# A decoder layer on one core: the MLP's norm transposes by two row tiles with pairs of column blocks, and six shared load places

## The chip, the cores and the metric

One core of a Trainium2 chip runs the whole kernel. The metric is device time in microseconds (us) of one execution, the median of several runs. TensorE (PE) multiplies and transposes, VectorE (DVE), ScalarE (ACT) and GpSimd (POOL) do elementwise work, and SyncE (SP) only issues transfers; POOL and ACT issue some too. Each engine and each queue works through its own instructions in order.

## The reference, cut to what matters

One decoder layer for 2048 tokens of width 1024, all in float32. Four token mixers (a gated MLP, a state-space layer, a gated recurrence and an attention with forget gates) come first and take about the first 1000 us; the change doesn't touch them. What follows them is

```python
x = x + group_rms_norm(y, mix_norm_g) @ w_out
h = rms_norm(x, norm2_g)
x = x + square(relu(h @ w_mlp_in)) @ w_mlp_out     # 1024 -> 4096 -> 1024
return rms_norm(x, final_g)
```

where rms_norm(x, g) is x / sqrt(mean(x^2) + 1e-6) * g by rows.

## The kernel before

A tile framework gives the instructions their order on each engine, from the program's order and from which tile buffers are free, and it adds the waits. In the stages ahead of the MLP, TensorE keeps the program's order; in the MLP (class MLP) all engines take the framework's.

**Precision.** Every matmul operand is split into a high and a low part (split, L54 on ACT and L58 on DVE): the high part is a cast, the low part the difference. A product is three matmuls: high x high, high x low, low x high (L1556 to L1558 and L1581 to L1583).

**Products by blocks.** Both MLP products use a seven-product scheme on 2 x 2 blocks (tables FIRST and SECOND): the operands of each of the seven are single blocks or sums and differences of two blocks. Where two are needed, both are loaded into one tile of [128, 2, 512] and POOL adds or subtracts them in place (united, L1484). For the first product five of the seven weights (all but numbers 4 and 3) and most of the token operands are such pairs. For the second product the sums of weights are written to memory beforehand (weight_sums), all but one, number 1.

**Steps.** The tokens are done in two halves of 1024 rows, the later rows first ("first half" below means the one done first). In each half there are two column parts (c) of the hidden width; in each part an IN block, seven products of 8 steps (order 1, 4, 5, 7, 3, 2, 6), and an OUT block, seven of 8 (order 3, 5, 6, 1, 2, 4, 7). So a half has 4 x 56 = 224 steps, each of 12 matmuls of 128x128 by 128x512. A step's weights are asked for two steps ahead (make(n + AHEAD)); in steps 1 to 5 of an IN product the token operands of the next product are loaded and split (tokens_side, four tiles).

**prep.** The MLP's first product wants the normalised tokens transposed. prep does this for one half: it loads x1 tiles of 128 rows x 1024 (L1462), ACT sums the squares (L1464), a chain of 12 small DVE operations gives the reciprocal root (rsqrt_, L28 to L36), DVE scales the rows in place (L1469), TensorE transposes blocks of 128x128 (L50), ACT moves four of them (a piece) at once out of PSUM and multiplies with the norm's weight (L1477) into one of two ht buffers, and SP stores that as hT (L1478). It does four row tiles at a time and one block of 128 columns (k) per transposed piece. It is a generator: every yield hands back to the caller. For the first half it runs beside the output projection (wout_jobs), one call per turn of it from the fifth on; the rest follows when those turns are used up. For the second half it runs inside the first half's steps: from step 11 on, one call in every second step (`if n % 2 and n > 10: next(more, None)`). Four tiles take 14 calls: one for the loads, six more until the first transposes, then one per k.

**Places.** Loads that need a pair, the token operands and the x1 tiles of prep all take their SBUF tile from one pool, m_raw, of 4 KB per partition and five places:

```python
self.raw = P("m_raw", 5)
xt = self.raw.tile([128, D], F32, tag="raw", name="h")           # prep
raw = self.raw.tile([128, 2, 512], F32, tag="raw", name="raw")   # load
```

Single weights have a pool of their own (m_rw, five places of 2 KB). A pair's place comes free when its high and low parts have been made (L54, L58); an x1 tile's place when its last block has been transposed.

**The end of a half.** finish (L1592) multiplies the rows of a finished row tile with the reciprocal root and with gf, the final norm's weight spread over all partitions. gf has a pool of its own and is loaded once, ahead of the MLP.

The functions that the diff touches and what calls them:

Of the kernel before, what the change touches and what calls it, by code (L numbers as in the profile page):

```python
# [1425 lines left out]
class MLP:  # L1426
# [4 lines left out]
    def __init__(self, tc, cst, final_g, x1, hT, w1, w2, S2, out, T=2048):  # L1431
        self.tc, self.nc, self.cst, self.x1, self.hT, self.w1, self.w2, self.out, self.T = tc, tc.nc, cst, x1, hT, w1, w2, out, T
        self.final_g, self.S2 = final_g, S2
        self.D, self.FF = w1.shape
        self.KD = self.D // 128
        self.HT = 1024
        self.NC = 2
        self.NP = self.FF // 128 // self.NC // 2
        self.es = ExitStack()
        self.P = lambda n, b, **k: self.es.enter_context(tc.tile_pool(name=n, bufs=b, reuse_waits="tile", **k))  # L1440
        P = self.P
        self.bp = P("m_b", 2)
        self.raw = P("m_raw", 5)
        self.rw = P("m_rw", 5)
        self.wp = P("m_w", 4)
        self.htp = P("m_ht", 2)
        self.sm = P("m_sm", 2)
        self.jkp = P("m_jk", 1)
        self.ps_i = P("m_psi", 3, space=PSUM)
        self.halves = list(reversed(range(T // self.HT)))  # L1450

    def prep(self, half):

        nc, D = self.nc, self.D
        for q in range(self.HT // 512):
            ss = self.sm.tile([128, 4], F32, tag="ss", name="ss")
            rs = self.sm.tile([128, 4], F32, tag="rs", name="rs")
            xs = []
            for j in range(4):
                r0 = half * self.HT + q * 512 + j * 128  # L1460
                xt = self.raw.tile([128, D], F32, tag="raw", name="h")
                nc.sync.dma_start(out=xt, in_=self.x1[r0 // 128])  # L1462
                jk = self.jkp.tile([128, D], BF16, tag="jk", name="jk")
                nc.scalar.activation(out=jk, in_=xt, func=AF.Square, accum_out=ss[:, j:j + 1])  # L1464
                xs.append(xt)
            yield
            rsqrt_(nc, self.sm, rs, ss, 1.0 / D, "n2")
            for j in range(4):
                nc.vector.tensor_scalar(out=xs[j], in0=xs[j], scalar1=rs[:, j:j + 1], scalar2=None, op0=MUL)  # L1469
            for _ in range(5):  # L1470
                yield
            for k in range(self.KD):
                pt = self.ps_i.tile([128, 512], F32, tag="pi", name="tp")
                for j, h in enumerate(xs):
                    transpose(nc, out=pt[:, j * 128:(j + 1) * 128], in_=h[:, k * 128:(k + 1) * 128], ident=self.cst["ident"])
                ht = self.htp.tile([128, 512], F32, tag="ht", name="ht")
                nc.scalar.activation(out=ht, in_=pt, func=AF.Copy, scale=self.cst["g2"][:, k:k + 1])  # L1477
                nc.sync.dma_start(out=self.hT[k][half * 2 + q], in_=ht)  # L1478
                yield

    def united(self, raw, sign):
# [12 lines left out]
    def tokens_side(self, half, i):  # L1494

        a, b, sign = FIRST[i][1]
        bh = self.bp.tile([128, 4, 512], F32R, tag="bh", name="bh")
        bl = self.bp.tile([128, 4, 512], F32R, tag="bl", name="bl")
        yield bh, bl
        for k in range(4):  # L1500
            raw = self.load([self.hT[4 * x[0] + k][half * 2 + x[1]] for x in (a, b) if x])
            split(self.nc, bh[:, k], bl[:, k], self.united(raw, sign if b else 0))
            yield

# [91 lines left out]
    def run(self):  # L1596
        nc, P, NP = self.nc, self.P, self.NP

        P("m_pad", 1).tile([128, 32], F32, tag="pad", name="pad")
        self.cp = P("m_c", 1)  # L1600
        self.sp = P("m_s", 3)
        self.shp = P("m_sh", 4)
        accp = P("m_acc", 1)
        gp = P("m_gf", 1)
        ps_o = P("m_pso", 5, space=PSUM)
        self.C, self.acc = {}, {}
        ends = {}
        for order, table, n in ((IN_ORDER, FIRST, 0), (OUT_ORDER, SECOND, 1)):
            seen, last = {}, {}
            for i in order:  # L1610
                for blk, _ in table[i][2]:
                    seen.setdefault(blk, i)
                    last[blk] = i
            ends[n] = {i: [b for b in seen if seen[b] == i] for i in order}, {i: [b for b in last if last[b] == i] for i in order}
        steps = [(half, c, out, i, p) for half in self.halves for c in range(self.NC) for out in range(2)
                 for i in (OUT_ORDER if out else IN_ORDER) for p in range(NP)]
        made, sides = {}, {}
        groups = [s[:4] for s in steps if s[4] == 0 and not s[2]]

        def side(n):  # L1620
            if n < len(groups):
                half, _, _, i = groups[n]
                g = self.tokens_side(half, i)
                sides[groups[n]] = next(g)
                return g
            return iter(())

        def make(n):
            if n >= len(steps):
                return  # L1630
            half, c, out, i, p = steps[n]
            if not out:
                made[n] = (self.first_weight(c, i, p),)
            else:
                made[n] = self.second_weight(c, i, p), self.hidden_side(i, p)

        gf = gp.tile([128, self.D], F32, tag="gf", name="gf")
        nc.sync.dma_start(out=gf, in_=self.final_g.partition_broadcast(128))
        for _ in side(0):
            pass  # L1640
        for n in range(AHEAD):
            make(n)
        nxt, more, part = 1, iter(()), iter(())
        sums = weight_sums(self.tc, self.w2, self.S2, 1, SP, nc.sync)
        for n, (half, c, out, i, p) in enumerate(steps):
            if c == 0 and not out and i == IN_ORDER[0] and p == 0:
                k = self.halves.index(half) + 1
                more = self.prep(self.halves[k]) if k < len(self.halves) else iter(())
            if c == 0 and not out and i == IN_ORDER[3]:
                self.acc[p] = accp.tile([128, self.D], F32, tag=f"acc{p}", name="acc")  # L1650
                with behind(self.tc, SP):
                    nc.sync.dma_start(out=self.acc[p], in_=self.x1[half * self.HT // 128 + p])
            if n % 2 and n > 10:
                next(more, None)
            if n > 7 * NP and n % 3 == 0:
                next(sums, None)
            make(n + AHEAD)
            if not out and p == 1:
                part = side(nxt)
                nxt += 1  # L1660
            if not out and 1 <= p < 6:
                next(part, None)
            got = made.pop(n)
            first, last = (e[i] for e in ends[out])
            if not out:
                self.product_in(i, p, got[0], sides[half, c, out, i], first, last)
                continue
            if p == 0:
                po = [ps_o.tile([128, 512], F32, tag="po", name="po") for _ in range(4)]
            self.product_out(p, *got, po)  # L1670
            if p == NP - 1:
                for t in range(4):
                    for (rt, d), sign in SECOND[i][2]:
                        self.gather(self.acc[4 * rt + t][:, d * 512:(d + 1) * 512], po[t], sign)
                    if c == self.NC - 1:
                        for rt in range(2):

                            if (rt, 0) in last and all((rt, 1) not in e for e in later(ends[1][1], i)) or \
                                    (rt, 1) in last and all((rt, 0) not in e for e in later(ends[1][1], i)):
                                self.finish(half, 4 * rt + t, gf)  # L1680
        self.es.close()
# [17 lines left out]
def hybrid_kernel(tc, A, out, T=2048):  # L1699
    nc = tc.nc  # L1700
    with ExitStack() as top:
# [8 lines left out]
                 zb=dp.tile([T, 256], F32, name="zb"), qk=dp.tile([2, 4, 2, 64, T], F32, name="qk"),  # L1710
                 v=dp.tile([T, 4, 2, 64], F32, name="v"), ys=dp.tile([T, 1024], F32, name="ys"),
                 negc=dp.tile([4, T], F32, name="negc"), x1=[dp.tile([128, 1024], F32, name=f"x1_{t}") for t in range(T // 128)],
                 hT=[[dp.tile([128, 512], F32, name=f"hT_{k}_{q}") for q in range(T // 512)] for k in range(8)])
        S2 = {(i, c): dp.tile([1024, 512], F32, name=f"s2_{i}{c}") for i in OUT_ORDER if SECOND[i][1][1] and i != 1 for c in range(2)}
        D5 = s5_scratch(dp)
        r8 = cp.tile([128, NPR], F32, name="r8")
# [115 lines left out]
```

## Time and profile before

| what | us |
|---|---|
| median of 3 runs | 2665.54 (2664.99 to 2669.57) |
| the profiled execution | 2665.58 |
| its span | 2663.4 |
| MLP: first product_in matmul | at 1127.78 |
| TensorE busy, of the span | 2248.9 |

Times in rows count from the span's start. An instruction's row gives its engine, its line in the kernel, what it writes and reads, and in square brackets how long its engine had stood idle before it and what ended that. PEclk, the granted clock, is the share of TensorE's full 2.4 GHz. The DMA share is the mean busy share of the core's 16 DMA engines.

### The profile page before, as it was taken

To read this page: it belongs to the slowest core of one execution; us is meant where nothing else is said; L and a number is where in the kernel's file an instruction comes from. 1 tells how busy PE (TensorE), PEld (TensorE's weight loads), DVE (VectorE), ACT (ScalarE), POOL (GpSimd) and SP (SyncE) were. 2 spreads that over 40 slices of the span, in tenths; PEclk is the share of its full clock that TensorE was granted. 3 is DMA by queue.
4 is the path that set the end of the run, shared out by engine and by line. 5 is a ranking of instruction groups with operands and counts; after the bars stand their busy time and mean duration, and the time that the engine had idled before them with its cause. 6 is when DMAs were issued, how large, how long until landed. Compare 5 with 4: busy or idle time off the path is not lost.

```text
span 2663.4 us, 32203 instructions
## 1 busy us (share of the span) xinstructions
PE 2248.9 (84%) x10077; PEld 1809.3 (68%) x10077; DVE 1699.7 (64%) x3776; ACT 1171.6 (44%) x2351; POOL 895.8 (34%) x956
## 2 busy tenths in 40 slices
PE   6788986985898978784474598999989999999997
PEld 5666765764776867563353376887877788788885
DVE  6776654753566755451152288687978779768797
ACT  4323443342555643341242243566445663356543
POOL 2133343230000011221111155346643467345561
PEclk9899998997899989896786698999999999999998
DMA  7434566445465546853442398687338963377423
GB/s 174 133 76 111 144 145 175 111 126 169 147 182 185 161 143 212 301 172 95 138 139 80 120 262 209 180 238 227 111 99 248 288 215 120 102 220 230 143 87 107
DMA packets 397147, 434.52 MB, mean 163 GB/s; under 512 B 42864, under 2 KB 277392, under 8 KB 396720
## 3 DMA queue, kind: packets, MB, share of 16 engines
q1 hardware_dynamic: 357840, 352.64, 43.8%
q0 software_dynamic: 30400, 65.15, 9.6%
q10 hardware_dynamic: 8736, 14.68, 1.7%
q8 instruction: 80, 1.31, 0.2%
q14 instruction: 91, 0.75, 0.1%
HBM read 369.30 MB, written 96.57 MB: 175 GB/s over the span
## 4 chain that ended last, share of the span: by engine, by line
PE 44%; DMA 15%; DVE 6%; issue 5%; POOL 5%; ACT 3%; SPq 2%; POOLq 0%; ACTq 0%; DVEq 0%
PE po L1581 6%; PE po L1582 6%; PE po L1583 6%; PE pi L1556 5%; PE pi L1558 5%; PE pi L1557 5%; DMA raw<-in_w_mlp_in_dram 5%; POOL raw L1484 3%; DMA q<-qk 3%; DVE wl L58 2%; DMA raw<-hT 2%; PE s L1087 2%; PE t L50 2%; PE po L1362 1%; PE po L1364 1%
## 5 line engine op out<-in xcount | busy, mean ns | idle before, releaser
L1484 POOL TENSOR_TENSOR raw<-raw 128x512 f32<-128x512 f32 x272 | 388.3, 1434 | 570.5 <-DMA raw<-in_w_mlp_in_dram 364.4
L1556 PE MATMUL pi<-bh,wh 128*128 128x512 f32 x896 | 378.0, 422 | 179.6 <-ACT wh L54 172.2
L58 DVE TENSOR_TENSOR wl<-raw,wh 128x512 fp32r<-128x512 f32 x448 | 403.7, 907 | 169.7 <-ACT wh L54 168.1
L1558 PE MATMUL pi<-bh,wl 128*128 128x512 f32 x896 | 372.9, 416 | 3.9 <-DVE wl L58 3.9
L1581 PE MATMUL po<-wh,sh 128*128 128x512 f32 x896 | 355.0, 396 | 20.0 <-DVE acc L1572 19.8
L1557 PE MATMUL pi<-bl,wh 128*128 128x512 f32 x896 | 370.7, 414 | 0.0
L54 ACT CAST wh<-raw 128x512 fp32r<-128x512 f32 x448 | 275.2, 616 | 211.8 <-POOL raw L1484 139.2
L1582 PE MATMUL po<-wl,sh 128*128 128x512 f32 x896 | 353.3, 394 | 4.5 <-DVE wl L58 4.5
L1583 PE MATMUL po<-wh,sl 128*128 128x512 f32 x896 | 350.1, 394 | 0.1
L1543 POOL TENSOR_TENSOR s<-c 128x512 f32<-128x512 f32 x160 | 254.4, 1604 | 270.6 <-DVE sl L58 243.2
L1556 PEld LDWEIGHTS pi<-bh,wh 128*128 128x128 f32 x896 | 181.8, 203 | 235.4 <-ACT wh L54 187.9
L58 DVE TENSOR_TENSOR sl<-s,sh 128x512 fp32r<-128x512 f32 x160 | 188.8, 1188 | 47.0 <-ACT sh L54 44.0
L1558 PEld LDWEIGHTS pi<-bh,wl 128*128 128x128 f32 x896 | 180.8, 202 | 52.7 <-DVE wl L58 14.7
L1581 PEld LDWEIGHTS po<-wh,sh 128*128 128x128 f32 x896 | 170.8, 191 | 60.4 <-DVE acc L1572 23.1
L54 ACT CAST sh<-s 128x512 fp32r<-128x512 f32 x160 | 99.4, 621 | 251.8 <-PE po L1582 202.7
L1557 PEld LDWEIGHTS pi<-bl,wh 128*128 128x128 f32 x896 | 182.2, 203 | 37.8
L1582 PEld LDWEIGHTS po<-wl,sh 128*128 128x128 f32 x896 | 171.1, 191 | 40.4 <-DVE wl L58 5.4
L1583 PEld LDWEIGHTS po<-wh,sl 128*128 128x128 f32 x896 | 170.8, 191 | 36.7 <-DVE sl L58 0.4
L436 PE MATMUL z<-wh,hl 128*128 128x512 f32 (+1 forms) x384 | 152.3, 397 | 16.7 <-ACT hl L54 8.5
L1572 DVE TENSOR_TENSOR c<-pi,c 128x512 f32<-128x512 f32 x128 | 87.5, 684 | 106.2 <-PE pi L1558 106.2
L58 DVE TENSOR_TENSOR bl<-raw,bh 128x512 fp32r<-128x512 f32 x112 | 101.9, 919 | 68.6 <-ACT bh L54 66.6
L438 PE MATMUL z<-wh,hl 128*128 128x512 f32 (+1 forms) x384 | 143.4, 373 | 1.6 <-DVE hl L58 1.6
(358 smaller groups left out, 4314.4 us busy)
## 6 DMA issues: line engine op xcount, KB each, us to landing
raw<-in_w_mlp_in_dram SPq DMA_DIRECT2D x384, 256.0 KB
raw<-hT SPq DMA_DIRECT2D x192, 256.0 KB
raw<-s SPq DMA_DIRECT2D x128, 256.0 KB
raw<-in_w_mlp_out_dram SPq DMA_DIRECT2D x128, 256.0 KB
x<-in_x_dram SPq DMA_DIRECT2D x32, 512.0 KB
s<-in_w_mlp_out_dram POOLq DMA_DIRECT2D x32, 512.0 KB, 8.1
x<-x POOLq DMA_DIRECT2D x31, 512.0 KB, 5.7
raw<-in_w_in_dram SPq DMA_DIRECT2D x32, 256.0 KB
```

The source lines that it names most:

```text
L54: nc.scalar.copy(out=hi, in_=src)
L58: nc.vector.tensor_tensor(out=lo, in0=src, in1=hi.bitcast(F32), op=SUB)
L436: nc.tensor.matmul(pz, lhsT=hi[:, k, sl], rhs=wh, start=(k == 0), stop=False)
L438: nc.tensor.matmul(pz, lhsT=lo[:, k, sl], rhs=wh, start=False, stop=(k == 7))
L1484: self.nc.gpsimd.tensor_tensor(out=raw[:, 0], in0=raw[:, 0], in1=raw[:, 1], op=ADD if sign > 0 else SUB)
L1543: self.nc.gpsimd.tensor_tensor(out=s, in0=src, in1=self.C[b[1], b[0], p], op=ADD if sign > 0 else SUB)
L1556: nc.tensor.matmul(pt, lhsT=wh[:, sl], rhs=bh[:, k], start=(k == 0), stop=False)
L1557: nc.tensor.matmul(pt, lhsT=wh[:, sl], rhs=bl[:, k], start=False, stop=False)
L1558: nc.tensor.matmul(pt, lhsT=wl[:, sl], rhs=bh[:, k], start=False, stop=(k == 3))
L1581: nc.tensor.matmul(po[t], lhsT=sh[:, ts], rhs=vh, start=(p == 0), stop=False)
L1582: nc.tensor.matmul(po[t], lhsT=sh[:, ts], rhs=vl, start=False, stop=False)
L1583: nc.tensor.matmul(po[t], lhsT=sl[:, ts], rhs=vh, start=False, stop=(p == self.NP - 1))
```

## The change

prep takes two row tiles at a time, and two blocks of columns per transposed piece: a piece is still four transposes and 128x512 elements, and a half still has 16 of them. The piece leaves PSUM through DVE, as a product with the norm's weight spread along the tokens. hT is laid out by 512 tokens and pairs of k, so that a piece is stored with rows of 256 tokens. Two tiles take 8 calls: one for the loads, three more until the first transposes, then one per k pair. The pool m_raw has six places, and gf has no pool any more: in each half it is loaded into a place of m_raw at the first step of the sixth OUT product of the second column part.

```diff
-        self.raw = P("m_raw", 5)
+        self.raw = P("m_raw", 6)
...
     def prep(self, half):
         nc, D = self.nc, self.D
-        for q in range(self.HT // 512):
-            ss = self.sm.tile([128, 4], F32, tag="ss", name="ss")
-            rs = self.sm.tile([128, 4], F32, tag="rs", name="rs")
+        g2 = self.cst["g2"].rearrange("p (k o) -> p k o", o=1)
+        for m in range(self.HT // 256):
+            ss = self.sm.tile([128, 2], F32, tag="ss", name="ss")
+            rs = self.sm.tile([128, 2], F32, tag="rs", name="rs")
             xs = []
-            for j in range(4):
-                r0 = half * self.HT + q * 512 + j * 128
+            for j in range(2):
                 xt = self.raw.tile([128, D], F32, tag="raw", name="h")
-                nc.sync.dma_start(out=xt, in_=self.x1[r0 // 128])
+                nc.sync.dma_start(out=xt, in_=self.x1[half * self.HT // 128 + m * 2 + j])
...
             yield
             rsqrt_(nc, self.sm, rs, ss, 1.0 / D, "n2")
-            for j in range(4):
+            for j in range(2):
                 nc.vector.tensor_scalar(out=xs[j], in0=xs[j], scalar1=rs[:, j:j + 1], scalar2=None, op0=MUL)
-            for _ in range(5):
+            for _ in range(3):
                 yield
-            for k in range(self.KD):
-                pt = self.ps_i.tile([128, 512], F32, tag="pi", name="tp")
-                for j, h in enumerate(xs):
-                    transpose(nc, out=pt[:, j * 128:(j + 1) * 128], in_=h[:, k * 128:(k + 1) * 128], ident=self.cst["ident"])
-                ht = self.htp.tile([128, 512], F32, tag="ht", name="ht")
-                nc.scalar.activation(out=ht, in_=pt, func=AF.Copy, scale=self.cst["g2"][:, k:k + 1])
-                nc.sync.dma_start(out=self.hT[k][half * 2 + q], in_=ht)
+            for k in range(0, self.KD, 2):
+                pt = self.ps_i.tile([128, 2, 256], F32, tag="pi", name="tp")
+                for kk in range(2):
+                    for j, h in enumerate(xs):
+                        transpose(nc, out=pt[:, kk, j * 128:(j + 1) * 128], in_=h[:, (k + kk) * 128:(k + kk + 1) * 128],
+                                  ident=self.cst["ident"])
+                ht = self.htp.tile([128, 2, 256], F32, tag="ht", name="ht")
+                nc.vector.tensor_tensor(out=ht, in0=pt, in1=g2[:, k:k + 2].to_broadcast([128, 2, 256]), op=MUL)
+                ts = slice(m % 2 * 256, (m % 2 + 1) * 256)
+                nc.sync.dma_start(out=self.hT[half * 2 + m // 2][k // 2][:, :, ts].rearrange("k p t -> p k t"), in_=ht)
                 yield
...
-            raw = self.load([self.hT[4 * x[0] + k][half * 2 + x[1]] for x in (a, b) if x])
+            raw = self.load([self.hT[half * 2 + x[1]][2 * x[0] + k // 2][k % 2] for x in (a, b) if x])
...
-        gp = P("m_gf", 1)
...
-        gf = gp.tile([128, self.D], F32, tag="gf", name="gf")
-        nc.sync.dma_start(out=gf, in_=self.final_g.partition_broadcast(128))
...
+            if p == 0 and c == self.NC - 1 and i == OUT_ORDER[5]:
+                gf = self.raw.tile([128, self.D], F32, tag="raw", name="gf")
+                nc.sync.dma_start(out=gf, in_=self.final_g.partition_broadcast(128))
...
-                 hT=[[dp.tile([128, 512], F32, name=f"hT_{k}_{q}") for q in range(T // 512)] for k in range(8)])
+                 hT=[[dp.tile([2, 128, 512], F32, name=f"hT_{q}_{k}") for k in range(4)] for q in range(T // 512)])
```

## Rows read from the trace of the kernel before

**Rows 1.** The page: the span, and busy time by engine.

```profile
span 2663.4 us, 32203 instructions
PE 2248.9 (84%) x10077; PEld 1809.3 (68%) x10077; DVE 1699.7 (64%) x3776; ACT 1171.6 (44%) x2351; POOL 895.8 (34%) x956
```

**Rows 2.** Stretches of the MLP: length, busy time (instructions) by engine, PEclk, DMA share, GB/s.

```profile
1127.00:1160.00 33.00, 31.86 (x128) 25.71 (x129) 22.12 (x21) 23.28 (x43) 16.44 (x12) 0.90 0.85 256
1160.00:1345.00 185.00, 102.87 (x320) 75.08 (x319) 49.51 (x85) 48.75 (x84) 30.43 (x24) 0.73 0.40 122
...
1358.00:1522.00 164.00, 80.24 (x212) 56.58 (x211) 43.38 (x70) 41.65 (x73) 33.36 (x26) 0.68 0.29 89
1522.00:1697.00 175.00, 163.29 (x692) 132.21 (x692) 137.32 (x155) 67.22 (x117) 89.33 (x68) 0.95 0.82 220
1697.00:1852.00 155.00, 153.46 (x675) 126.19 (x674) 118.15 (x153) 101.68 (x178) 86.94 (x60) 1.00 0.79 234
...
2014.00:2177.00 163.00, 156.19 (x677) 125.88 (x676) 131.67 (x208) 106.65 (x188) 90.68 (x66) 1.00 0.90 272
2177.00:2337.00 160.00, 154.19 (x673) 126.80 (x672) 130.86 (x157) 64.98 (x114) 76.53 (x49) 0.98 0.36 115
```

**Rows 3.** Groups of instructions between 1160 and 1520: busy, mean ns, idle before.

```profile
L1556 PE MATMUL pi<-bh,wh 128*128 128x512 f32 x181 | 97.0, 536 | 164.7 <-ACT wh L54 164.7
...
L1484 POOL TENSOR_TENSOR raw<-raw 128x512 f32<-128x512 f32 x48 | 61.3, 1276 | 298.9 <-DMA raw<-in_w_mlp_in_dram 217.3 <-DMA raw<-hT 73.8 <-DVE c L1572 5.1
```

**Rows 4.** Timelines of SP, POOL, ACT and DVE, 1204 to 1220: start, length, instruction.

```profile
1205.41 0.94 SPq L1491 DMA_DIRECT2D raw<-in_w_mlp_in_dram  x2
1212.04 0.81 SPq L1491 DMA_DIRECT2D raw<-hT  x2
...
1209.37 1.26 POOL L1484 TENSOR_TENSOR raw<-raw 128x512 f32<-128x512 f32 x1 [5.96 <-DMA raw<-in_w_mlp_in_dram]
...
1210.67 0.62 ACT L54 CAST wh<-raw 128x512 fp32r<-128x512 f32 x1 [6.01 <-POOL raw L1484]
...
1211.32 0.69 DVE L58 TENSOR_TENSOR wl<-raw,wh 128x512 fp32r<-128x512 f32 x1 [5.93 <-ACT wh L54]
```

**Rows 5.** Timeline of SP: prep's loads of x1 tiles, and a store.

```profile
1145.41 3.37 SPq L1462 DMA_DIRECT2D h<-x  x3
...
1352.16 0.43 SPq L1478 DMA_DIRECT2D hT<-ht  x1
1352.69 1.95 SPq L1462 DMA_DIRECT2D h<-x  x4
```

**Rows 6.** Timeline of SP in the second half: every second tile's issue.

```profile
2155.78 0.93 SPq L1491 DMA_DIRECT2D raw<-in_w_mlp_in_dram  x2
...
2159.29 0.93 SPq L1491 DMA_DIRECT2D raw<-in_w_mlp_in_dram  x2
```

**Rows 7.** A stretch of the second half, columns as in rows 2.

```profile
2050.00:2100.00 50.00, 50.00 (x221) 41.17 (x221) 33.99 (x43) 26.34 (x46) 27.60 (x21) 1.00 1.01 303
```

**Rows 8.** Single operations: tile ht (min/median/max ns), tile h, the page's groups, DVE's timeline.

```profile
L1477 ACT ACTIVATE ht<-tp,g x32: 671/687/702, 1061.1 to 1549.0; 128x512 f32<-128x512 f32 x32
...
L1469 DVE TENSOR_SCALAR h<-h,rs x16: 744/748/1756, 1056.6 to 1370.7; 128x1024 f32<-128x1024 f32 x16
...
L1572 DVE TENSOR_TENSOR c<-pi,c 128x512 f32<-128x512 f32 x128 | 87.5, 684 | 106.2 <-PE pi L1558 106.2
...
1088.16 0.17 DVE L28 TENSOR_SCALAR n2m<-ss 128x4 f32<-128x4 f32 x1 [4.34 <-ACT jk L1464]
```

**Rows 9.** The chain that ended last, between 1095 and 1130: start, length, what.

```profile
1100.06 0.44 PE tp L50 x4
...
1103.95 0.44 PE tp L50 x4
...
1110.17 4.74 DMA hT<-ht
...
1115.73 3.65 DMA hT<-ht
```

## The prediction

> **What bounds the kernel now.** I began with the page: TensorE is busy for 84% of the span [rows 1], an average over unlike stages. A table of stretches cut at the MLP's blocks comes next [rows 2]. The MLP is four pairs of an IN block (product_in, 56 steps of 12 matmuls) and an OUT block (product_out, 56 steps). The reader should compare blocks that do the same work. IN of the first half, first column part, runs from 1127 to 1522, 395 us; the same block of the second half, which has no prep beside it, takes 163, and the IN block after it in the first half 155. In most of the 395 TensorE is busy for about half the time at a granted clock of 0.73 and 0.68 (part of the time at 1.2 instead of 2.4 GHz), where the other IN blocks have 1.00. Nothing else in the MLP is so far from its twin: OUT takes 175 against 160.
>
> Next I asked what that stretch waits for [rows 3]. TensorE's idle time, 164.7 us, ends with the cast of a weight; POOL, which adds the two halves of a weight pair, stands idle for 298.9 of 360 us, almost all of it waiting for a load. DMA is not short there: its share is 0.40 and 0.29 [rows 2]. So follow one load [rows 4]: SP issues it at 1205.41, the sum begins at 1209.37, the cast at 1210.67, the subtraction at 1211.32 and ends at 1212.01, and at 1212.04 SP issues the next. One load place is going round, 6.63 us per tile, and 48 pair loads [rows 3] times 6.63 are 318 of the 360 us. Where the other four are, the SP queue shows [rows 5]: prep of the other half took them for its four x1 tiles from 1145, the last transposed piece left at 1352.16, and 0.5 us later SP loads the next four. The bound is thus SBUF places held by prep, through all of IN.
>
> **The change, part by part.** Durations are from one execution, 2665.58 us around a span of 2663.4 [rows 1], 0.04 us above the median shown; the sum is made against 2665.58.
>
> *Places.* Prep holds two of six instead of four of five, so loads get four. Prep lasts longer in steps: a pair of tiles takes 8 calls where four took 14, one call per two steps, so 64 steps from step 11 instead of 56, and ends in OUT. What IN then costs, built up: a fed block, 155. Transposes: calls 5 to 8, 13 to 16 and 21 to 23 fall into IN, 11 of 16 pieces of four, at 0.44 us a piece [rows 9]: 5 us. Entry: 128 matmuls in the first 33 us where a full stretch (675 in 155) would have 144 [rows 2], 4 us. That is 164. Now the places. With five, tiles come every 1.76 us [rows 6], so a place's turn is at most 8.8 us, and at least the 6.63 of a lone load; four places then give a tile every 1.66 to 2.2 us. A group with paired weights wants 12 tiles in 8 steps, 22.1 us of matmuls (155/56 each) and 0.9 of transposes; the places give them in 20 to 26. I take 1.5 us of loss for each of some 4.5 groups, 7. At each change of pair the next two x1 tiles may be loaded some three steps before the old two go, leaving two places; two changes in IN at 4 us, 8. IN by the places: 179.
>
> DMA as a check: the second half's IN moved 272 GB/s for 163 us, 44 MB [rows 2]; prep loads and stores its 1024 rows of 4 KB once each, 8.4 MB, about 11/16 of it in IN: 50 MB. At 272 that is 184 us; at 303, the rate of its busiest 50 us at a share of 1.01 [rows 7], 165. Both limits hold, so I take the later, 184; bounds 165 and 215 (the second is the first rival's): **-211 us**. The Trainium skill's DMA: Bandwidth & Descriptors (Bandwidth) puts the limit of HBM traffic per core near 358 GB/s, by which those 50 MB would need an estimated 140 us and DMA would not matter; the row shows the engines full at 303, so the row decides.
>
> *Eviction.* The transposed piece, 687 ns on ACT, becomes a DVE product from PSUM; the nearest row is the DVE sum of the same shape from PSUM, 684 ns [rows 8]. In IN DVE has room (132 busy of 163 in the fed twin) and ACT is relieved by the same amount; nothing there. VectorE: DVE Perf Modes (Specifications and the cycle table) in the Trainium skill speaks against the move: ScalarE sits closer to PSUM, and its formulas give an estimated 658 ns on VectorE against 570 on ScalarE. The trace disagrees; by the page the move would cost 32 x 88 ns, 3 us of DVE time in all.
>
> *Norm arithmetic.* Squares and scalings stay eight per half; the 12 small rsqrt operations, 0.17 us each [rows 8], run eight times instead of four: 2 us more DVE per pair of tiles at most, hidden in IN as above.
>
> *OUT, first part.* Five transposed pieces, two scalings and one rsqrt chain now fall into it: 5 x 0.68 + 1.5 + 2 = 7 us of DVE, which is busy for 137 of 175 there [rows 2] and leads TensorE by its weight splits. The old pieces there were ACT's. Of the 7 I take 5, bounds -10 and 12, since this block's 15 us over its twin may shrink too: **+5**.
>
> *The first prep, beside the output projection.* TensorE is in program order there. A call comes every 1.95 us (two between 1100.06 and 1103.95 [rows 9]); the last group moves from call 28 to call 32, 8 us later, if the tail shows. Against it, the old tail waits 4.74 us for a store to free one of two ht buffers and 3.65 for the last store [rows 9], and six places let x1 tiles come earlier. Bounds -5 and +8, I take **+2**. Stores have rows half as long; the same bytes, the nearest row is the store above, taken as equal.
>
> *Final norm's scale.* Its load leaves the crowded start and stands in SP's queue before OUT's sixth group, eight steps (over 20 us) ahead of its use. OUT's last two groups load single sums through other places, so no pair waits: 0. It gives up its place at the half's last norm, and from then on loads have six: the second half's IN can go from 163 towards 155; I take **-3**, bounds 0 and -8.
>
> Sum: -211 + 5 + 2 - 3 = -207; 2665.58 - 207 = **2459**.
>
> **Rivals.**
> *Two places, not four:* SP runs ahead and loads the next pair of x1 tiles as soon as places are free, so four are held as before, and two remain. For it: SP did load at once in [rows 5]. Against: x1 loads stand in program order among the pair loads. Then 48 tiles at 3.3 us are 159, with 33 before and 22 for the eight steps of the unpaired group (2.77 each), transposes beneath: IN 215, total 2490. Chance 0.17.
>
> *TensorE-bound:* places and DMA suffice, IN 165, OUT as before, -5 at the start, -8 later: 2665.6 - 230 - 13 = 2423. For it: the fed blocks run on five places at clock 1.00. Chance 0.15.
>
> *SP's queue stops at each change of pair:* an x1 load that has no place holds every load behind it until the old pair is transposed, three times three turns of 6.63: IN 244, total 2519. For it: one queue issues everything. Against: with six places it seldom finds none. That would be the change not doing what it says. Chance 0.07.
>
> *Slower:* DVE now stands in the chain of prep. It works in order; a piece waits there for a free ht buffer, that for a store, and the store stands in SP's queue behind loads that wait for places which only DVE's subtractions free. The price of a block would be two turns of 6.63 and a store of 4.7: 18 us, sixteen times, 288: total 2747. It decides the sign from 207/16 = 13 us per block. For it: the start shows ACT held 4.74 us in this way. Against: in IN a call comes every two steps, 5.5 us, longer than a store takes, and there are two buffers. Chance 0.03.
>
> **How the numbers follow.** My forecast has 0.58. The range takes it with its bounds and the first two rivals: from 2412 (2423 with OUT 10 shorter, rounded down) to 2520, which takes in the third rival too; the first with OUT at +12 and the start at +8 is 2665.6 - 180 + 20 = 2506. These cases hold 0.97 of the chance, and I count that a fifth of it may lie past their bounds, since each block's loss is a guess between bounds. A measurement can tell about 0.2%, 5 us, from no change. All cases but the last are faster by far more: faster 0.96, within 0.2% 0.01, slower 0.03.
>
> **What would show it.** Right: the stretch from the first product_in to the first product_out is 165 to 215 us, its clock near 1.00, its DMA share about 0.9; SP issues pair loads every 2 us or so, with x1 tiles two at a time; the ht product on DVE is near 0.68 us; the fed blocks are unchanged. Wrong: pair sums still spaced by over 3 us, idle DVE in front of the ht product, or OUT longer than 187 us.

## The result, and the profile after

| what | before | changed |
|---|---|---|
| median, us | 2666.11 (4 runs) | 2460.85 (2460.28 to 2463.03, 4 runs) |
| ratio to before | 1 | 0.923, 95% interval 0.9214 to 0.9246 |
| span of the profiled execution, us | 2663.4 | 2461.0 |

The change takes 205 us off; 207 were forecast, and 2459 against 2460.85. The two profiled executions differ by 202 us in span, since the one of the changed kernel is the slowest of its four (2463.03). The parts of the sum are less exact than their total, as the stretches show. The page of the changed kernel answers to [rows 1]: TensorE does the same 10077 instructions in 202 us less span.

```profile
span 2461.0 us, 32297 instructions
PE 2196.6 (89%) x10077; PEld 1780.3 (72%) x10077; DVE 1755.3 (71%) x3856; ACT 1148.6 (47%) x2319; POOL 899.4 (37%) x956
```

The MLP's blocks in the changed kernel, cut within 1.5 us of the first matmul of each, columns as in [rows 2]:

```profile
1129.80:1326.20 196.40, 174.67 (x717) 137.01 (x718) 153.77 (x211) 113.53 (x200) 89.80 (x65) 0.91 0.82 252
1326.20:1498.00 171.80, 161.70 (x688) 130.68 (x687) 147.47 (x173) 65.87 (x116) 89.80 (x70) 0.96 0.86 231
1498.00:1655.50 157.50, 155.71 (x683) 127.60 (x683) 123.07 (x156) 103.52 (x183) 86.73 (x60) 1.00 0.80 232
1655.50:1813.00 157.50, 152.77 (x667) 125.64 (x666) 133.62 (x204) 66.87 (x118) 74.44 (x49) 0.99 0.37 117
1813.00:1975.00 162.00, 155.50 (x677) 126.09 (x676) 136.24 (x208) 107.20 (x190) 93.94 (x67) 1.00 0.93 279
```

The first IN block went from 395 us to 196, at a granted clock of 0.91 instead of 0.73 and 0.68, a DMA share of 0.82 instead of 0.40 and 0.29. The OUT block behind it, from first matmul to first matmul, is 173 instead of 175, and the OUT block of the second column part 159.1 instead of 162.5. The rest hardly moved. From here on "IN" and "OUT" without more are these first two blocks.

What IN waits for, the groups of instructions between 1130 and 1326 (the answer to [rows 3]):

```profile
L1559 PE MATMUL pi<-bh,wh 128*128 128x512 f32 x224 | 94.0, 420 | 16.8 <-ACT wh L54 7.9 <-ACT bh L54 3.2 <-DVE c L1575 3.1
...
L1487 POOL TENSOR_TENSOR raw<-raw 128x512 f32<-128x512 f32 x62 | 85.5, 1383 | 97.2 <-DMA raw<-in_w_mlp_in_dram 67.9 <-DMA raw<-hT 19.9 <-DVE wl L58 2.0
```

TensorE's idle time before the first matmuls of the triples (L1559) is 16.8 us where it was 164.7, and POOL's 97.2 where it was 298.9. The timeline of SP shows prep's loads, two x1 tiles at a time, and the stores of pieces next to them (the answer to [rows 5]):

```profile
1152.60 2.02 SPq L1462 DMA_DIRECT2D h<-x  x2
...
1214.52 0.37 SPq L1481 DMA_DIRECT2D hT<-ht  x1
...
1216.43 0.85 SPq L1462 DMA_DIRECT2D h<-x  x2
...
1272.45 0.92 SPq L1462 DMA_DIRECT2D h<-x  x2
1274.85 0.37 SPq L1481 DMA_DIRECT2D hT<-ht  x1
...
1313.48 0.46 SPq L1494 DMA_DIRECT2D raw<-in_w_mlp_in_dram  x1
1314.43 1.16 SPq L1462 DMA_DIRECT2D h<-x  x2
...
1335.61 0.38 SPq L1481 DMA_DIRECT2D hT<-ht  x1
```

The second pair is loaded 2 us after the last piece of the first was sent to store, the third 2.4 us before the last piece of the second: up to there places are hardly held twice. The fourth pair is loaded at 1314.43, 21 us before the last piece of the third, so from there prep does hold four places. IN's last weight pair had been asked for just before (1313.48), so this falls to OUT, which asks for few pairs. The piece leaves through DVE in the same time as it did through ACT [rows 8]:

```profile
L1479 DVE TENSOR_TENSOR ht<-tp,g x32: 676/682/693, 1062.5 to 1377.1; 128x512 f32<-128x512 f32 x32
```

And at the MLP's start, the chain that ended last: the last piece is transposed at 1122.04, 11 us later than before (1110.56, the first line, from TensorE's timeline of the kernel before), but no store holds the chain any more (it was 4.74 and 3.65 us, [rows 9]); one load of hT does.

```profile
1110.56 0.60 PE L50 MATMUL tp<-ident,h 128*128 128x128 f32 x4
...
1122.04 0.45 PE tp L50 x4
...
1124.01 3.74 DMA raw<-hT
```

### The profile page after: what moved, and what is told of

Its sections match the earlier page's. It is cut to its first block, busy times and chain, and to the rows that moved or that the text cites. A ratio compares the mean times of both kernels' runs of the same rounds, so it can differ in the third digit from the quotient of the medians.

```text
span 2461.0 us, 32297 instructions
## 1 busy us (share of the span) xinstructions
PE 2196.6 (89%) x10077; PEld 1780.3 (72%) x10077; DVE 1755.3 (71%) x3856; ACT 1148.6 (47%) x2319; POOL 899.4 (37%) x956
## 4 chain that ended last, share of the span: by engine, by line
PE 47%; DMA 11%; DVE 7%; issue 5%; POOL 3%; ACT 2%; SPq 1%; POOLq 0%; ACTq 0%; DVEq 0%
PE po L1584 7%; PE po L1585 7%; PE po L1586 7%; PE pi L1559 6%; PE pi L1561 6%; PE pi L1560 6%; DMA q<-qk 3%; DVE wl L58 2%; POOL raw L1487 2%; PE s L1087 2%; PE t L50 2%; DMA raw<-in_w_mlp_in_dram 2%; PE po L1362 2%; DMA ngc<-negc 2%; PE po L1364 1%
## 5 line engine op out<-in xcount | busy, mean ns | idle before, releaser
L1487 POOL TENSOR_TENSOR raw<-raw 128x512 f32<-128x512 f32 x272 | 394.1, 1455 | 384.4 <-DMA raw<-in_w_mlp_in_dram 222.7
L1559 PE MATMUL pi<-bh,wh 128*128 128x512 f32 x896 | 357.1, 399 | 24.5 <-ACT wh L54 8.5
L1561 PE MATMUL pi<-bh,wl 128*128 128x512 f32 x896 | 354.2, 395 | 5.9 <-DVE wl L58 5.9
L1560 PE MATMUL pi<-bl,wh 128*128 128x512 f32 x896 | 353.5, 394 | 3.4 <-DVE bl L58 3.3
L58 DVE TENSOR_TENSOR sl<-s,sh 128x512 fp32r<-128x512 f32 x160 | 196.7, 1236 | 48.5 <-ACT sh L54 48.4
L1559 PEld LDWEIGHTS pi<-bh,wh 128*128 128x128 f32 x896 | 170.9, 191 | 69.3 <-ACT wh L54 10.5
L1561 PEld LDWEIGHTS pi<-bh,wl 128*128 128x128 f32 x896 | 170.7, 190 | 45.8 <-DVE wl L58 9.9
L1560 PEld LDWEIGHTS pi<-bl,wh 128*128 128x128 f32 x896 | 170.8, 191 | 39.2 <-DVE bl L58 4.6
L1102 ACT ACTIVATE p<-p,ng 128x512 f32<-128x512 f32 (+3 forms) x160 | 103.7, 651 | 88.1 <-DVE ng L1098 88.0
L437 PE MATMUL z<-wl,hl 128*128 128x512 f32 (+1 forms) x384 | 143.9, 375 | 0.6 <-DVE wl L388 0.6
```

Of the source, the lines that this page charges most:

```text
L58: nc.vector.tensor_tensor(out=lo, in0=src, in1=hi.bitcast(F32), op=SUB)
L1487: self.nc.gpsimd.tensor_tensor(out=raw[:, 0], in0=raw[:, 0], in1=raw[:, 1], op=ADD if sign > 0 else SUB)
L1559: nc.tensor.matmul(pt, lhsT=wh[:, sl], rhs=bh[:, k], start=(k == 0), stop=False)
L1560: nc.tensor.matmul(pt, lhsT=wh[:, sl], rhs=bl[:, k], start=False, stop=False)
L1561: nc.tensor.matmul(pt, lhsT=wl[:, sl], rhs=bh[:, k], start=False, stop=(k == 3))
```

## The experiments

All are compared by the IN block of one profiled execution each and by the ratio of their times to the kernel before. Executions differ by some us ahead of the MLP (the first output-projection matmul starts between 630 and 638 us in these profiles), which the blocks leave out. Lengths of blocks in the text go from first matmul to first matmul; some of the rows are cut up to 2 us beside that. A yardstick is the second half's first IN block, which hardly depends on the edits: it takes 160.8 to 162.8 us in the twelve profiles without a seventh place. So a difference of 2 or 3 us in one block says nothing by itself.

**How many places are left for loads.** Three runs change only that. The first has the old prep, four tiles at a time, with six places: two are left.

```diff
-        self.raw = P("m_raw", 5)
+        self.raw = P("m_raw", 6)
...
-        gp = P("m_gf", 1)
...
+            if p == 0 and c == self.NC - 1 and i == OUT_ORDER[5]:
+                gf = self.raw.tile([128, self.D], F32, tag="raw", name="gf")
```

> The old prep (four tiles at a time, piece out through ACT) with six places and the final norm's scale in one of them: two places are left for loads. Places theory: a lone load's turn of 6.6 us over two places gives a tile every 3.3 us, up to 4.4 with the crowded turn of 8.8; 48 pair tiles then take 159 to 211 us, first IN block 215 to 250 us, total 2480 to 2515. Rival (what counts is that prep takes two tiles at a time, not how many places are left): IN stays above 300 us and the total above 2570.

Measured: 2522.08 us, 0.9445 (0.9427 to 0.9463). IN is within what the places theory expected, the total 7 us above it. Its IN block:

```profile
1134.23:1381.90 247.67, 195.25 (x708) 146.59 (x708) 127.86 (x184) 119.32 (x209) 82.52 (x64) 0.86 0.64 195
```

The sixth place alone, with the old prep, brings some 145 of the 205 us. Without the 33 us of entry and the 22 of unpaired steps, as in the prediction, 193 us are left for 48 pairs, 4.0 us each, a turn of 8.0 us where a lone load's took 6.63. That is a mean of unlike stretches. SP's timeline in this run, where with two places every second issue is the same place's, early and late in IN:

```profile
1186.12 0.81 SPq L1491 DMA_DIRECT2D raw<-hT  x2
1192.47 0.81 SPq L1491 DMA_DIRECT2D raw<-hT  x2
...
1305.67 0.94 SPq L1491 DMA_DIRECT2D raw<-in_w_mlp_in_dram  x2
1313.74 0.93 SPq L1491 DMA_DIRECT2D raw<-in_w_mlp_in_dram  x2
```

A turn is 6.4 us early, as with the lone place, and 8.1 late. Why it grows no run shows.

The second has the new prep in five places, with a place of its own for the norm's scale: three are left.

```diff
-        self.raw = P("m_raw", 6)
+        self.raw = P("m_raw", 5)
...
+        gp = P("m_gf", 1)
...
+        gf = gp.tile([128, self.D], F32, tag="gf", name="gf")
+        nc.sync.dma_start(out=gf, in_=self.final_g.partition_broadcast(128))
...
-            if p == 0 and c == self.NC - 1 and i == OUT_ORDER[5]:
-                gf = self.raw.tile([128, self.D], F32, tag="raw", name="gf")
-                nc.sync.dma_start(out=gf, in_=self.final_g.partition_broadcast(128))
```

> The changed prep with five places and a place of its own for the final norm's scale: three places are left for loads. Places theory: a tile every 2.2 to 2.9 us, 27 to 35 us for a group that wants 12 tiles and has 23 us of matmuls: first IN block 205 to 230 us against 196 with six, total 2470 to 2495. DMA rival (with three or more places the transfers themselves are the limit): IN within 4 us of 196, total within 5 us of 2461.

Measured: 2471.24 us, 0.9259 (0.9239 to 0.9279). IN is 4 us longer than with six places, less than the places theory asked for and at the edge of the other; the total, 10 us longer, is past the 5 us of that other:

```profile
1128.95:1329.70 200.75, 173.69 (x717) 134.66 (x718) 142.82 (x210) 111.84 (x196) 84.50 (x63) 0.94 0.80 242
```

The third has seven places; five are left.

```diff
-        self.raw = P("m_raw", 6)
-        self.rw = P("m_rw", 5)
+        self.raw = P("m_raw", 7)
+        self.rw = P("m_rw", 3)
```

> The changed kernel with seven shared places and three instead of five places for single weights (for room). Places theory: five places for loads as in the blocks without prep, first IN block 184 to 192 us. DMA or DVE theory: IN 194 to 199. OUT blocks, which use the single-weight places, may get longer by some us each; the verdict is the IN block's.

Measured: 2459.36 us, 0.9222 (0.9202 to 0.9241), no different from the change: IN is 9 us shorter, and OUT, which lives on the places for single weights that were taken away, 12 us longer.

```profile
1129.07:1316.00 186.93, 168.39 (x716) 135.49 (x717) 147.91 (x217) 113.64 (x199) 89.66 (x65) 0.94 0.87 264
1316.00:1500.00 184.00, 163.13 (x691) 130.34 (x690) 148.43 (x167) 66.81 (x116) 91.93 (x70) 0.94 0.82 216
```

So IN by places left for loads is 395, 248, 201, 196, 187 us for one to five. The first two have the old prep and the other three the new one: the step from one to two is the places' alone, the step from two to three is that of places and prep together, and no run parts them. From three on each place gives little, and something else holds most of what is left above a block without prep.

**The burst of loads.** In the changed kernel's IN block the worst stretch is this, in windows of 5 us:

```profile
1215.00:1220.00 5.00, 5.00 (x24) 4.15 (x23) 4.00 (x5) 3.78 (x8) 1.93 (x2) 1.00 0.73 247
1220.00:1225.00 5.00, 2.97 (x14) 2.12 (x12) 2.76 (x7) 4.84 (x10) 0.39 (x1) 0.99 1.06 362
1225.00:1230.00 5.00, 2.82 (x6) 1.81 (x7) 4.90 (x10) 3.06 (x6) 3.10 (x3) 0.50 1.09 359
1230.00:1235.00 5.00, 2.96 (x10) 2.02 (x8) 4.93 (x8) 1.22 (x2) 2.95 (x3) 0.82 0.91 293
1235.00:1240.00 5.00, 4.01 (x10) 3.14 (x10) 1.63 (x2) 1.17 (x3) 0.39 (x1) 0.52 0.34 107
1240.00:1245.00 5.00, 3.05 (x8) 1.95 (x7) 2.87 (x5) 3.22 (x6) 0.00 (x0) 0.50 0.10 25
```

From 1220 to 1245 TensorE does 44 matmuls, where a full stretch has 110 (221 in 50 us, [rows 7]). (The rows' own counts add up to 48, since a matmul across a border counts in both windows; the expectation below took them, and 120 for the full stretch.) The second pair of x1 tiles, issued at 1216.43, meets the last four of the eight acc loads of half a megabyte that belong to this product (1214.94 to 1229.36); DMA's share is over 1 for 10 us, weights come late, and TensorE goes on at 1.2 GHz (granted clock 0.50) after 3.6 us idle.

Two rows say that this is not the whole of the stall. From 1235 on DMA is nearly idle (0.34 and 0.10), while SP stands in front of loads of hT for a place that a weight's subtraction on DVE frees, 10.5 us in two waits, both after 1231:

```profile
1230.99 12.60 SPq L1494 DMA_DIRECT2D raw<-hT  x4
SPq L1494 <- DVE wl L58: 10.5, 2, 5.9
```

And in the second half of the kernel before, where prep holds no place, acc loads of the same size fill DMA just as much without stopping TensorE:

```profile
2050.00:2055.00 5.00, 5.00 (x23) 4.14 (x23) 2.58 (x4) 2.28 (x4) 2.42 (x2) 1.00 1.17 311
...
2085.00:2090.00 5.00, 5.00 (x24) 4.15 (x23) 3.00 (x4) 2.28 (x5) 2.59 (x2) 1.00 1.10 359
```

So by these rows the burst alone does not stop TensorE; it does so where prep's loads, work and places come on top. The run moves the acc loads one product on:

```diff
-            if c == 0 and not out and i == IN_ORDER[3]:
+            if c == 0 and not out and i == IN_ORDER[4]:
```

> The changed kernel with the eight half-megabyte acc loads moved from the IN block's fourth product to its fifth, whose weights come unpaired. DMA theory: the burst that stops TensorE between 1220 and 1245 (48 of 120 matmuls) goes: first IN block 180 to 187 us, second half's IN not longer, total 2444 to 2453. Places theory: a load's turn is not much shorter, IN 193 to 199, total within 5 us of 2461.

Measured: 2453.41 us, 0.9199 (0.9174 to 0.9224); the interval meets that of the change, so by time alone it isn't settled. IN is 7 us shorter, just past the expected 180 to 187, and the window from 1220 to 1245 now holds 83 matmuls where it held 44:

```profile
1127.81:1316.80 188.99, 167.31 (x716) 132.62 (x717) 160.47 (x216) 115.54 (x203) 88.95 (x65) 0.96 0.87 263
...
1220.00:1245.00 25.00, 20.89 (x83) 15.89 (x82) 23.94 (x37) 18.73 (x34) 7.20 (x5) 0.93 0.68 229
```

Both edits at once (seven places, three for single weights, acc later) ask whether they mend the same stall.

```diff
-        self.raw = P("m_raw", 6)
-        self.rw = P("m_rw", 5)
+        self.raw = P("m_raw", 7)
+        self.rw = P("m_rw", 3)
...
-            if c == 0 and not out and i == IN_ORDER[3]:
+            if c == 0 and not out and i == IN_ORDER[4]:
```

> The run with seven shared places (and three for single weights) and the acc loads in the fifth instead of the fourth product. Alone the first took 9 us off the first IN block and the second 7. If they mend different stalls: IN 178 to 182 us. If they mend the same stall: IN 185 to 189.

Measured: 2454.34 us, 0.9203 (0.9186 to 0.9221), and IN 184 us, between the two answers but nearer to the second: 12 us together where the single edits gave 9 and 7. OUT, at 187 us, gives it back. The stall itself answers more clearly: from 1210 to 1255, where a full stretch has 199 matmuls, the changed kernel does 130, the run with seven places 154, with acc later 177, with both 192. The three runs of the next part that leave prep's steps and the acc loads where they were do 125, 129 and 140, so the stall is no accident of one execution.

```profile
1125.17:1309.20 184.03, 166.10 (x717) 133.21 (x718) 151.94 (x218) 113.04 (x199) 91.68 (x65) 0.95 0.88 269
```

**DVE in the chain of prep.** Three runs. In the first the piece leaves through ACT again.

```diff
-                nc.vector.tensor_tensor(out=ht, in0=pt, in1=g2[:, k:k + 2].to_broadcast([128, 2, 256]), op=MUL)
+                for kk in range(2):
+                    nc.scalar.activation(out=ht[:, kk], in_=pt[:, kk], func=AF.Copy, scale=self.cst["g2"][:, k + kk:k + kk + 1])
```

> The changed kernel with the transposed piece leaving PSUM through ACT again, as two activations of 128x256, one for each column block. If DVE's place in the chain of prep costs time: first IN block 4 to 10 us shorter, first OUT block 3 to 6 us shorter, total 2446 to 2455. If not: total within 5 us of 2461.

Measured: 2461.85 us, 0.9223 (0.9201 to 0.9246): no difference. IN is 200 us (4 longer), OUT 172 (173 in the change); no cost of DVE's place in the chain is to be seen.

The small reciprocal-root chain looked like the miss. In the changed kernel's IN block the groups of DVE hold

```profile
L32 DVE TENSOR_TENSOR n2t<-n2y 128x2 f32<-128x2 f32 x9 | 5.6, 627 | 0.3
...
L36 DVE SCALAR_TENSOR_TENSOR n2y<-n2t,n2y 128x2 f32<-128x2 f32 x6 | 5.0, 838 | 0.1
L35 DVE SCALAR_TENSOR_TENSOR n2t<-n2t,n2m 128x2 f32<-128x2 f32 x9 | 4.7, 518 | 0.2
```

that is, operations of 0.16 us with means of 0.5 to 0.8, and the chains in IN (three, and the first steps of a fourth) take 19.1 us where I had put 2 each. The next run puts the chain on POOL, but for two integer steps:

```diff
-            rsqrt_(nc, self.sm, rs, ss, 1.0 / D, "n2")
+            rsqrt_(nc, self.sm, rs, ss, 1.0 / D, "n2", eng=nc.gpsimd)
```

> The changed kernel with prep's small reciprocal-root chain on POOL, all but its two integer steps. In the changed kernel's first IN block three such chains take 19.1 us of DVE (steps of 0.16 us stretch to 1.2 while POOL adds), against 5.5 for two before. If that is the term the forecast had too small: first IN block 186 to 191 us against 196, DVE's steps of the chain under 1 us in all, total 2450 to 2456. If DVE's time there is covered: IN 194 to 200, total within 5 us of 2461.

Measured: 2467.9 us, 0.926 (0.9239 to 0.928), 7 us above the change, and IN 196 us: nothing gained. By itself that is not conclusive, since POOL now has 45 operations more in IN (110 for 65) and DVE waits for the chain's result. The second run shortens the chain instead, leaving out two of three Newton rounds:

```diff
-def rsqrt_(nc, pool, out, ss, inv_n, nm, eng=None):
+def rsqrt_(nc, pool, out, ss, inv_n, nm, eng=None, rounds=3):
...
-    for i in range(3):
+    for i in range(rounds):
...
-        o = out if i == 2 else y
+        o = out if i == rounds - 1 else y
...
-            rsqrt_(nc, self.sm, rs, ss, 1.0 / D, "n2")
+            rsqrt_(nc, self.sm, rs, ss, 1.0 / D, "n2", rounds=1)
```

> The changed kernel with one Newton round instead of three in prep's reciprocal root (two rounds left out: 6 small DVE steps in place of 12, and a coarser root). If the chain's 19.1 us of DVE in the first IN block cost time there: DVE's steps of the chain fall to about 8 us, IN 186 to 191 us, total 2451 to 2456. If they are covered: IN 194 to 199, total within 5 us of 2461.

Measured: 2456.45 us, 0.9204 (0.918 to 0.9229), its runs scattered from 2444 to 2462. The chain takes 7.2 us of DVE in IN (the six groups of its rows summed) where it took 19.1, and IN hardly answers; at 194 us it lies, like the total, at the border of the two expectations:

```profile
1131.56:1325.30 193.74, 170.63 (x716) 134.64 (x717) 142.44 (x194) 113.95 (x200) 93.75 (x66) 0.94 0.85 256
```

2.7 us for 12 us of DVE, no more than a block scatters: the stretched chain is real, but nearly all of it lies beside other waits. As the term that the forecast missed it is out.

**Prep out of the IN block.** OUT loads mostly through other places, all but its product 1, so prep can run there. First, from step 57 on, the piece leaving through ACT:

```diff
-            if n % 2 and n > 10:
+            if n % 2 and n > 7 * NP:
...
-                nc.vector.tensor_tensor(out=ht, in0=pt, in1=g2[:, k:k + 2].to_broadcast([128, 2, 256]), op=MUL)
+                for kk in range(2):
+                    nc.scalar.activation(out=ht[:, kk], in_=pt[:, kk], func=AF.Copy, scale=self.cst["g2"][:, k + kk:k + kk + 1])
```

> The changed kernel with the second half's prep started in the first OUT block (step 57 instead of 11), where no load shares the places with it, and the piece leaving through ACT. Places and DMA theory: the first IN block comes down to its twin's time, 158 to 165 us; the OUT block takes the transposes, four chains and eight scalings, 176 to 195 us against 172; total 2430 to 2450. Rival (the first IN block is long for reasons of its own, its start beside the output projection's end): IN above 180 us, total above 2450.

Measured: 2445.4 us, 0.917 (0.9156 to 0.9184), faster than the change. IN 164 us, OUT 178; the IN block behind it is 164 us (155 in the change), and prep's last four calls reach into it:

```profile
1129.11:1293.30 164.19, 156.58 (x673) 126.79 (x674) 132.82 (x164) 107.61 (x189) 94.86 (x66) 0.97 0.93 276
...
1293.00:1470.00 177.00, 162.35 (x716) 130.72 (x715) 140.16 (x202) 78.96 (x148) 85.30 (x65) 0.97 0.85 227
1472.00:1634.00 162.00, 155.43 (x680) 126.96 (x679) 126.58 (x155) 105.78 (x189) 90.77 (x64) 0.98 0.83 240
```

The same with the acc loads later (the diff is against that run):

```diff
-            if c == 0 and not out and i == IN_ORDER[3]:
+            if c == 0 and not out and i == IN_ORDER[4]:
```

> As the run before, and the acc loads in the fifth instead of the fourth product of the IN block. If their burst costs time only beside prep: within 4 us of the run before. If it costs by itself: 4 to 10 us less.

Measured: 2448.63 us (2438.07 to 2453.55), 0.9175 (0.9154 to 0.9196), with IN at 162 us (its profile is of the execution of 2438): within 4 us of the run before. Without prep in IN, moving the acc loads gains nothing that shows.

Then all 32 calls inside OUT, four in seven steps, with the acc loads where they were (the diff is against the run from step 57):

```diff
-            if n % 2 and n > 7 * NP:
+            if out and n % 7 % 2 == 0:
```

> Prep of the second half wholly inside the first OUT block, 32 calls in its 56 steps (four in seven), the piece leaving through ACT. If the IN block after it was 7 us longer in the run with prep from step 57 because prep's tail reached into it: that block back to 154 to 158 us, first IN block 162 to 167, OUT 178 to 186, total 2436 to 2444. If OUT can't take the last eight calls for free: OUT above 186 and total 2445 or more.

Measured: **2435.87 us, 0.9133 (0.911 to 0.9155)**, the best of all and at the lower end of what was expected: IN 162, OUT 181, and the IN block after it back at 155.

```profile
1126.06:1288.40 162.34, 156.37 (x672) 127.20 (x673) 130.45 (x159) 107.19 (x188) 96.85 (x67) 0.97 0.95 282
...
1290.00:1468.00 178.00, 163.74 (x726) 132.88 (x725) 142.64 (x205) 82.97 (x158) 86.26 (x64) 0.96 0.83 228
1470.00:1626.00 156.00, 154.28 (x677) 126.13 (x676) 121.60 (x154) 103.18 (x183) 92.42 (x64) 1.00 0.86 247
```

And with the piece through DVE, so that against the changed kernel only the condition differs:

```diff
-            if n % 2 and n > 10:
+            if out and n % 7 % 2 == 0:
```

> As the run before, but the piece leaves through DVE as in the changed kernel, so only the calls' steps differ from it. If DVE is what sets the pace in OUT: its 16 pieces of 0.68 us cost 5 to 11 us against the run before. If it is covered: within 4 us of it.

Measured: 2437.63 us, 0.9142 (0.9119 to 0.9165): the same, with IN at 161 us and OUT at 179. One line on top of the change is worth about 1%.

## Why the prediction was right, and where its parts were not

By its own steps, from the first matmul of each block (before 1127.78, 1522.1, 1697.4; after 1129.8, 1326.2, 1499.2), against spans of 2663.4 and 2461.0:

| step | forecast | measured |
|---|---|---|
| start of the MLP | +2 | +2 |
| first IN block | -211 | -198 |
| first OUT block | +5 | -2 |
| all that follows | -3 | -4 |
| sum | -207 | -202 |

*What bounds it.* Right. One place going round was the bound: the run with two places for loads and nothing else of prep changed takes IN from 395 to 248 us. The rest came with the new prep, which leaves four.

*IN: right in kind, 12 us too short.* 184 was forecast, 196 came. The floor of 164, with 5 us of transposes in it, was a little low, since its fed block of 155 is one of the second column part: the runs with prep elsewhere show 161 to 164 for this block, without the transposes. The term that failed is the one for places and pair changes, 7 + 8 us, and with it the DMA check that set 184: above 161 to 164 and the 5 of transposes IN has 27 to 30 us. The reason given for the 8 hardly occurred, since at both changes of pair that were counted places were held twice for at most 2.4 us. What cost there was a stall that begins where x1 and acc loads come together and in which SP then waits for places: moving acc saves 7 us, a fifth place 9, both 12. Of the 32 us between 196 and 164, 12 are these and 5 the transposes; the other 15 stay without a shown cause, and DVE's chain is not one by more than 3. An estimate that fits: with both edits IN moves the bytes that the DMA check counted (269 GB/s for 184 us are 49.5 MB, against 50), at its 272 GB/s and in its 184 us; without prep it is 45.8 MB (282 GB/s for 162 us), and the 3.7 MB between are 14 us at 269. No run tells bytes from the rest.

*OUT: 7 us too long.* I charged 5 of 7 us of added DVE work, and 2 us less than before came, no more than a block scatters. The run with the piece through ACT has the same OUT, and a whole prep's 16 pieces in OUT cost the same through either engine (181 and 179). DVE is busy for 147 of 172 us there and still covers them.

*Start: right by luck.* Stages ahead of the change ran 5.6 us later in this execution, as they scatter between all these profiles; take that off, and the start is 3.6 us earlier, not 2 later. The last piece came 11 us later, 6 of them from those stages, so 5 and not 8 from its later call; and the two waits for stores went, by which the step from the last output-projection matmul to the first of the MLP fell from 7.4 to 3.6 us.

*All that follows: right in size, not in place.* The second half's IN is 161 (162 before), not 160. Most of the 4 us lie in the OUT block before it (159.1, 162.5 before). With a seventh place that IN is 159 in both runs that have one, so more places may shorten it a little; that the sixth gave nothing because the scale holds one until the half's last norm is a guess.

*The rivals.* Two places instead of four didn't happen; where two places were made, the price was higher than I gave it (248, not 215), since the lone load's turn that I took holds in part of the block only. SP's queue did not stop at pair changes: in front of x1 loads it waited 2.0 us at most. But in the stall right behind one it stood for 10.5 us in front of loads of hT. The TensorE-bound rival's 165 did not come with prep in IN (196), only with prep out of it (161 to 164). The slower rival is refuted by the ACT run: the piece's place on DVE costs nothing measurable, let alone 13 us a block.

## What to carry to other kernels

When a stretch is slow while DMA and all engines have room, follow one buffer from issue to issue: if the next issue comes as the last reader ends, count the buffers and who holds the others. Here the second free place was worth 147 us and the fifth 9. A burst of loads that left TensorE running in one block (24 matmuls in 5 us) stopped it in another where prep's loads and places came on top, so look at both together. And before adding places, ask whether the holder can run in a stage that doesn't use them: one line for that was worth another 23 us here.

## What was not expected of the hardware

Small DVE operations stretch under POOL. In the changed kernel, DVE's timeline has steps of two SBUF inputs and two columns that last as long as a POOL sum beside them, where they take 0.16 us alone; the operation out of PSUM between them keeps its 0.68:

```profile
1284.60 1.24 DVE L32 TENSOR_TENSOR n2t<-n2y 128x2 f32<-128x2 f32 x1
1285.88 1.22 DVE L35 SCALAR_TENSOR_TENSOR n2t<-n2t,n2m 128x2 f32<-128x2 f32 x1
1287.01 0.68 DVE L1575 TENSOR_TENSOR c<-pi,c 128x512 f32<-128x512 f32 x1
```

The Trainium skill's SBUF — State Buffer (SBUF: two separate sides) has this as a rule: VectorE and GpSimd share a port pair, and a VectorE operation with two SBUF inputs and a GpSimd operation that reads SBUF exclude each other. The trace agrees, 0.16 us against 1.2, beside POOL's sums:

```profile
1284.09 1.74 POOL L1546 TENSOR_TENSOR s<-c 128x512 f32<-128x512 f32 x1
1285.79 2.52 POOL L1487 TENSOR_TENSOR raw<-raw 128x512 f32<-128x512 f32 x2
```

I had costed the chain from a row where POOL was idle.

What DMA moves at a share of about 1 depends on the loads. I took 303 GB/s at a share of 1.01 as full [rows 7], but that is a mean of unlike parts: windows of 5 us in it have 264 and 311 GB/s before the acc loads (2050 to 2060), and 342 to 359 at 1.09 to 1.11 with them (2080 to 2100). Acc loads have rows of 4 KB, weight pairs rows of 512 bytes; the mean packet is 613 bytes from 2050 to 2065 and 1100 from 2085 to 2100. In the changed kernel the burst reaches 362 at 1.06. The Trainium skill's DMA: Bandwidth & Descriptors (Bandwidth), which I set aside with its 358 GB/s, is close to these peaks; as a mean over an IN block no run here passed 283.
